# Delta net: learning rate and chunk decay spread over the heads by one float32r pass over stacked high and low rows

## The chip, the core and the metric

The kernel runs on one core of a Trainium2 chip. Its engines work side by side, each through its own list of instructions in order, and wait for each other by semaphores: PE (matrix products; its weight loads are shown as PEld), DVE (vector), ACT (scalar functions), POOL (GpSimd, a slower vector engine), and SP, which here only issues DMAs. The metric is the device time of one execution in microseconds, as the median of several. A lower number is better.

## The reference

The model has two blocks of two layers. The change is in the gated delta net ("GDN"), one of three mixers in each of the two layers of the second block, so it runs twice. There are 256 tokens, 8 heads of 64 channels and chunks of 64 tokens. What matters of it:

```python
def chunk_gated_delta_rule(q, k, v, g, beta):
    ...
    gc = jnp.cumsum(g, axis=-1)
    gamma = jnp.exp(jnp.where(causal, gc[..., :, None] - gc[..., None, :], -jnp.inf))
    kb = k * beta[..., None]
    m = jnp.where(strict, jnp.einsum('bnhid,bnhjd->bnhij', kb, k) * gamma, 0.0) + jnp.eye(c, dtype=jnp.float32)
    rhs = jnp.concatenate([v * beta[..., None], kb * jnp.exp(gc)[..., None]], axis=-1)
    sol = lax.linalg.triangular_solve(m, rhs, left_side=True, lower=True, unit_diagonal=True)
    ...
    q_dec = q * jnp.exp(gc)[..., None]
    k_dec = k * jnp.exp(gc[..., -1:] - gc)[..., None]
    chunk_dec = jnp.exp(gc[..., -1])
```

Per head and token there is one learning rate `beta` and one decay `exp(gc)`. Both multiply all 64 channels of their head. That is the "spreading" that the change is about.

## The kernel before

**Stages.** One program computes everything: the first block (to about 1120 us), then two delta-net layers. A layer (`layer`, L1846) runs the RWKV mixer and behind it the GDN mixer. The projections that other mixers need are cut into small pieces, and `fill()` puts such a piece between the steps of a mixer, so that PE has work while a mixer's chain goes through other engines. The order of each engine's list comes from a scheduler that estimates durations; it is fixed when the program is built.

**Weights.** Weights arrive in f32 (tile `wv`, DMA at L347). ACT casts them to float32r (`wh`, L375), DVE computes what the cast lost (`wl`, L376, called the residual below), and PE multiplies three times (L390, L391, L392). In the rows PE's operands all read f32, whether the matmul is full f32 or float32r. A full f32 matmul shows two records per instruction, a float32r one has one.

**Spreading before.** In `gdn`, `rows[32:40]` holds beta, 8 heads by 256 tokens. L1575 copies it into `b0`, a tile with the tag `inv_xt`; L1573 writes `eg`, the decay, in 8 rows of `alog`. A tag is a place in SBUF: a new tile with the tag waits until the readers of the former tile there are done. `selp` (tag `rw_e`, DVE copy at L1599) is a selector of 8 rows with ones where an output channel belongs to a head. The matmuls at L1603 (for `b0`) and L1652 (for `eg`), four each, contract over the 8 rows and give each channel its head's number, in full f32. L1604 and L1653 then multiply keys and queries by that.

**Inverses.** Both mixers solve a triangular system by `inverse_blocks` (L1165). The blocks go out by DMA and come back in `inv_t`; POOL then works through a chain of 30 small steps (L1184 a product, L1186 a sum), turns the result round into `inv_xt` (L1187), and DMAs carry it out (L1189) and back into place (L1197, tiles `rw_k`, `rw_v` and others, from `blocks`).

**RWKV's columns.** `column_tile` (L1272) takes 14 pieces of projection. Each has a tile `z` with the tag `rw_z`, two buffers in turn: POOL clears its first column (L1277), ACT fills it (L1278), DVE reads it (L1279). After the last column tile nothing else used `rw_z`.

**Around the change.** GDN's projection `gdn_proj` runs as fill work within RWKV: POOL clears three columns of `proj` (L1527), ACT copies (L1528) and scales (L1531), DVE convolves (L1533). RWKV's masks (L1418, L1419, DVE) follow scores on PE (L1415), whose next ones wait for them. L1242 and L1243 (ACT) take a logarithm of head sums and an exponential.

Of the kernel before, what the change touches and what calls it, by code (L numbers as in the profile page):

```python
# [11 lines left out]
F32 = mybir.dt.float32  # L12
F32R = mybir.dt.float32r
# [248 lines left out]
class Core:  # L262
# [1280 lines left out]
    def gdn(self, pool, i, c, qkv, gz, rows, alog, out, fill):  # L1543
        nc = self.nc
# [24 lines left out]
        df = self.sb(pool, [8, 4, 64], F32, "rw_ta", 2)  # L1569
        nc.vector.tensor_tensor(df, gcc[:, :, 63:64].to_broadcast([8, 4, 64]), gcc, op=ALU.subtract)  # L1570
        nc.scalar.activation(rows[64:72], df.rearrange("p c t -> p (c t)"), AF.Exp)
        eg = alog[:8]
        nc.scalar.activation(eg, gc, AF.Exp)  # L1573
        b0 = self.sb(pool, [8, 256], F32, "inv_xt")
        nc.vector.tensor_copy(b0, rows[32:40])  # L1575
        col = self.sb(pool, [128, 2, 72], F32, "rw_wa")
        p = self.psum()[:, :144].rearrange("p (c n) -> p c n", c=2)
        for cc in range(2):
# [16 lines left out]
        unit(k, 1.0, ("rw_k", "rw_v"))  # L1595
        fill()
        kb = self.sb(pool, S4, F32, "rw_lora")
        selp = self.sb(pool, [8, 4, 128], F32, "rw_e")
        nc.vector.tensor_copy(selp.rearrange("p n (h d) -> p (n h) d", h=2), self.ident[:8, :8, None].to_broadcast([8, 8, 64]))  # L1599
        for j in range(2):  # L1600
            p = self.psum().rearrange("p (n t) -> p n t", n=2)
            for n in range(2):
# [4 lines left out]
        both = self.sb(pool, [128, 2, 16, 64], F32, "rw_bkt")  # L1607
        gam, gat = both[:, 0], both[:, 1]
        selh = self.ident[:8, :8, None].to_broadcast([8, 8, 64])
        for cc in range(2):  # L1610
            p = self.psum().rearrange("p (h t) -> p h t", h=8)
# [36 lines left out]
        for j in range(2):  # L1648
            s = slice(2 * j, 2 * j + 2)
            p = self.psum().rearrange("p (n t) -> p n t", n=2)  # L1650
# [12 lines left out]
        for cc in range(2):  # L1663
            for src, o, w in ((v, vb, bcol), (k, ke, ecol)):
                p = self.psum()
# [9 lines left out]
        for ck in range(4):  # L1675
# [5 lines left out]
            if ck:  # L1681
# [3 lines left out]
                for hh in range(2):  # L1685
                    s = slice(64 * hh, 64 * hh + 64)
                    p = self.psum("acc").rearrange("p (n d) -> p n d", n=8)[rw, :4]
# [6 lines left out]
            p = self.psum("acc").rearrange("p (h d) -> p h d", h=8)[rw]  # L1694
# [4 lines left out]
            p = self.psum("acc").rearrange("p (n t) -> p n t", n=8)[:, :4]  # L1699
            for n in range(4):  # L1700
                for hh in range(2):
                    h = 2 * n + hh
# [6 lines left out]
            if ck < 3:  # L1709
                p = self.psum("acc").rearrange("p (n t) -> p n t", n=8)[:, :4]  # L1710
                for n in range(4):
                    for hh in range(2):
                        h = 2 * n + hh
# [648 lines left out]
```

## Time and profile before

| | us |
|---|---|
| runs | 3164.83, 3170.68, 3172.57 |
| median | 3170.68 |
| profiled execution, its own time | 3173.02 |
| its span, first to last instruction | 3171.1 |
| PE busy, PEld busy | 3062.1 (97%), 2569.1 (81%) |
| DVE, ACT, POOL busy | 2395.3 (76%), 1873.1 (59%), 151.4 (5%) |
| mean granted TensorE clock | 0.985 |

The profile is of one execution. An engine's busy time says how long it was working, not whether anyone waited for it; the chain of work is read from the rows of the timeline. There, a bracket at a row's end names how long its engine had been idle before and which instruction let it go on. Matmuls overlap in the pipeline, so their distance is read from start to start. The granted clock is a share of full speed: 1.00 is 2.4 GHz, 0.50 is 1.2 GHz.

### The profile page before, as it was taken

The numbers are of one execution on the slowest core, as the hardware profiler recorded it, in microseconds if no ns is written. First come the engines' busy times: TensorE is split into PE (matmuls) and PEld (weight loads), VectorE is DVE, ScalarE is ACT, GpSimd is POOL, SyncE is SP. The second block draws the span as 40 slices with busy tenths as digits, with TensorE's granted clock in tenths as the row PEclk, the third lists the DMA queues.
The fourth block names the chain that finished last, engine by engine and source line by source line (L and its number), as shares of the span: only waits on it lengthen the run. The fifth ranks groups of instructions, "written<-read, shape, count | busy, mean of one in ns | idle before, by whom it ended". The sixth has DMA issues, their size and how long they took to land. (4 is left out here: it accounts for less than half of the span.)

```text
span 3171.1 us, 48734 instructions
## 1 busy us (share of the span) xinstructions
PE 3062.1 (97%) x18724; PEld 2569.1 (81%) x18724; DVE 2395.3 (76%) x3811; ACT 1873.1 (59%) x2801; POOL 151.4 (5%) x285
## 2 busy tenths in 40 slices
PE   8988999999999989999999999999999999999998
PEld 7877688888878878888887888977888888888886
DVE  7677776766776677666666777579888888888886
ACT  5546555555455555545555555456777777777774
POOL 0000000000000011100000201000000000000000
PEclk9999999999999989999999999999999999999999
DMA  8425284451356134346843433488999999999993
GB/s 314 173 62 154 93 299 166 182 194 52 121 189 246 68 106 133 92 127 198 305 160 103 128 113 98 130 314 344 352 371 367 360 381 369 363 377 370 363 385 132
DMA packets 161085, 701.63 MB, mean 221 GB/s; under 512 B 41344, under 2 KB 55488, under 8 KB 97872
## 3 DMA queue, kind: packets, MB, share of 16 engines
q1 hardware_dynamic: 153984, 673.25, 58.4%
q0 software_dynamic: 6576, 24.98, 2.6%
q8 instruction: 148, 2.42, 0.3%
q14 instruction: 89, 0.73, 0.1%
q10 hardware_dynamic: 288, 0.25, 0.0%
HBM read 678.48 MB, written 19.94 MB: 220 GB/s over the span
## 5 line engine op out<-in xcount | busy, mean ns | idle before, releaser
L376 DVE TENSOR_TENSOR wl<-wv,wh 128x1024 fp32r<-128x1024 f32 (+1 forms) x808 | 970.5, 1212 | 380.4 <-ACT wh L375 369.4
L375 ACT CAST wh<-wv 128x1024 fp32r<-128x1024 f32 (+1 forms) x808 | 836.6, 1039 | 683.1 <-issue 207.7
L415 PE MATMUL bank<-xx,wh 128*128 128x512 f32 x1760 | 627.5, 399 | 5.1 <-ACT wh L375 2.4
L376 DVE TENSOR_TENSOR wx<-wv,ww 128x2048 fp32r<-128x2048 f32 x224 | 505.9, 2288 | 20.0 <-ACT ww L375 16.4
L416 PE MATMUL bank<-xx,wl 128*128 128x256 f32 x1760 | 494.0, 281 | 0.1
L375 ACT CAST ww<-wv 128x2048 fp32r<-128x2048 f32 x224 | 418.2, 1905 | 6.8 <-PE bank L392 3.8
L415 PEld LDWEIGHTS bank<-xx,wh 128*128 128x128 f32 x1760 | 331.2, 188 | 85.9 <-ACT wh L375 3.3
L390 PE MATMUL bank<-xx,wh 128*128 128x256 f32 x1120 | 338.9, 303 | 18.7 <-DVE xx L386 8.1
L416 PEld LDWEIGHTS bank<-xx,wl 128*128 128x128 f32 x1760 | 333.3, 189 | 5.3 <-DVE wl L376 0.6
L392 PE MATMUL bank<-xx,wl 128*128 128x256 f32 x1120 | 329.9, 295 | 7.0 <-DVE wl L376 6.9
L391 PE MATMUL bank<-xx,wh 128*128 128x256 f32 x1120 | 329.1, 294 | 0.0
L390 PEld LDWEIGHTS bank<-xx,wh 128*128 128x128 f32 x1120 | 222.4, 199 | 31.3 <-issue 17.8
L392 PEld LDWEIGHTS bank<-xx,wl 128*128 128x128 f32 x1120 | 222.6, 199 | 12.2 <-DVE wl L376 8.5
L391 PEld LDWEIGHTS bank<-xx,wh 128*128 128x128 f32 x1120 | 222.5, 199 | 6.1 <-issue 4.2
L390 PE MATMUL bank<-ww,xx 128*128 128x512 f32 x448 | 185.3, 414 | 0.0
L391 PE MATMUL bank<-wx,xx 128*128 128x512 f32 x448 | 178.1, 397 | 0.0
L441 PE MATMUL bank<-wh,hh 128*128 128x512 f32 x440 | 173.3, 395 | 4.6 <-ACT hh L375 4.5
L392 PE MATMUL bank<-ww,xx 128*128 128x512 f32 x448 | 177.4, 396 | 0.0
L390 PE MATMUL bank<-wh,xx 128*128 128x512 f32 x448 | 176.2, 393 | 0.0
L391 PE MATMUL bank<-wl,xx 128*128 128x512 f32 x448 | 175.8, 392 | 0.0
L392 PE MATMUL bank<-wh,xx 128*128 128x512 f32 x448 | 175.1, 391 | 0.0
L442 PE MATMUL bank<-wl,hh 128*128 128x512 f32 x440 | 172.2, 392 | 0.2 <-DVE wl L376 0.2
(667 smaller groups left out, 5363.8 us busy)
## 6 DMA issues: line engine op xcount, KB each, us to landing
wv<-in_moe_dram SPq DMA_DIRECT2D x336, 1024.0 KB, 7.2
wv<-in_ffn_dram SPq DMA_DIRECT2D x120, 1024.0 KB, 5.1
wv<-in_ffn_d_dram SPq DMA_DIRECT2D x30, 1024.0 KB, 5.7
wv<-in_in_t_dram SPq DMA_DIRECT2D x48, 512.0 KB, 3.7
wv<-in_in_g_dram SPq DMA_DIRECT2D x34, 512.0 KB, 4.1
wv<-in_in_r_dram SPq DMA_DIRECT2D x28, 512.0 KB, 3.7
wv<-in_ffn_dram SPq DMA_DIRECT2D x24, 512.0 KB, 4.5
wv<-in_br_dram SPq DMA_DIRECT2D x24, 512.0 KB, 4.0
```

Source lines behind the costliest of these rows:

```text
L375: self.nc.scalar.copy(h, v)
L376: self.nc.vector.tensor_sub(l, v, h)
L390: mm(out, l[0], r[0], start=start, stop=False)
L391: mm(out, l[0], r[1], start=False, stop=False)
L392: return mm(out, l[1], r[0], start=False, stop=stop)
L415: mm(out, w[0][:, k], self.xx[:, k], start=n == 0, stop=False, skip_group_check=True)
L416: mm(out[:, :256], w[1][:, k], self.xh[:, k], start=False, stop=n == nk - 1, skip_group_check=True)
L441: mm(p, x[0][:, s], w[0][:, c:c + n], start=first and r == 0, stop=False)
L442: mm(p, x[0][:, s], w[1][:, c:c + n], start=False, stop=False)
```

## The change

Each of `eg` and `b0` gets a new tile `both` of 40 rows in float32r, with the tag `rw_z`. POOL clears it, ACT casts the 8 rows into rows 0 to 7, and DVE writes what the cast lost into rows 32 to 39. The selector has 40 rows too, the same 8 at 0 and at 32; POOL clears and writes it, and DVE's copy falls away. One float32r matmul over 40 rows adds up the high and low parts. The number of matmul instructions is the same, and so are the tiles behind them.

```diff
@@ -1569,10 +1569,19 @@
         df = self.sb(pool, [8, 4, 64], F32, "rw_ta", 2)
         nc.vector.tensor_tensor(df, gcc[:, :, 63:64].to_broadcast([8, 4, 64]), gcc, op=ALU.subtract)
         nc.scalar.activation(rows[64:72], df.rearrange("p c t -> p (c t)"), AF.Exp)
+
+        spread = []
         eg = alog[:8]
         nc.scalar.activation(eg, gc, AF.Exp)
         b0 = self.sb(pool, [8, 256], F32, "inv_xt")
         nc.vector.tensor_copy(b0, rows[32:40])
+        for t in (eg, b0):
+            both = self.sb(pool, [40, 256], F32R, "rw_z", 2)
+            nc.gpsimd.memset(both.bitcast(F32), 0.0)
+            nc.scalar.copy(both[:8], t)
+            nc.vector.tensor_sub(both[32:40], t, both[:8].bitcast(F32))
+            spread.append(both)
+        eg, b0 = spread
         col = self.sb(pool, [128, 2, 72], F32, "rw_wa")
         p = self.psum()[:, :144].rearrange("p (c n) -> p c n", c=2)
         for cc in range(2):
@@ -1595,8 +1604,11 @@
         unit(k, 1.0, ("rw_k", "rw_v"))
         fill()
         kb = self.sb(pool, S4, F32, "rw_lora")
-        selp = self.sb(pool, [8, 4, 128], F32, "rw_e")
-        nc.vector.tensor_copy(selp.rearrange("p n (h d) -> p (n h) d", h=2), self.ident[:8, :8, None].to_broadcast([8, 8, 64]))
+        selp = self.sb(pool, [40, 4, 128], F32R, "rw_e")
+        nc.gpsimd.memset(selp.bitcast(F32), 0.0)
+        for n in (0, 32):
+            nc.gpsimd.tensor_copy(selp[n:n + 8].rearrange("p n (h d) -> p (n h) d", h=2),
+                                  self.ident[n:n + 8, n:n + 8, None].to_broadcast([8, 8, 64]))
         for j in range(2):
             p = self.psum().rearrange("p (n t) -> p n t", n=2)
             for n in range(2):
```

Line numbers up to L1571 are the same in both kernels; in the changed one the clear is L1580, the cast L1581, the residual L1582, and the lines behind move by 2, then by 9, then by 12.

On POOL, during RWKV's inverse in the first layer. Before (`rw_z_11995` and `rw_z_12030` are the tiles of RWKV's last two column tiles):

```order
L1277 MEMSET rw_z_11995 128x1
L1277 MEMSET rw_z_12030 128x1
L1184 ISA
L1184 TENSOR_TENSOR inv_m_11659<-inv_t_11653,inv_x_11655 128x15
L1186 TENSOR_TENSOR inv_x_11655<-inv_x_11655,inv_m_11659 128x15
L1184 TENSOR_TENSOR inv_m_11659<-inv_t_11653,inv_x_11655 128x28
```

After (`rw_z_13241` is the new tile for the decay):

```order
L1277 MEMSET rw_z_11995 128x1
L1277 MEMSET rw_z_12030 128x1
L1184 ISA
L1184 TENSOR_TENSOR inv_m_11659<-inv_t_11653,inv_x_11655 128x15
L1580 MEMSET rw_z_13241 40x256
L1186 TENSOR_TENSOR inv_x_11655<-inv_x_11655,inv_m_11659 128x15
L1184 TENSOR_TENSOR inv_m_11659<-inv_t_11653,inv_x_11655 128x28
```

The clear of the new tile, which takes the buffer of `rw_z_11995`, stands in the midst of the inverse, between its first product and its first sum. The clear of the second tile stands further down in the same chain; in the second layer both stand behind it.

On ACT, in the first layer, where GDN's projection begins. Before (`wh` and `wv` are weights, `proj` is GDN's projection, `rw_d` is RWKV's gate):

```order
L375 CAST wh_12204<-wv_12202 128x1024
L1399 COPY rw_d_12051<-bank_12052 128x512
L1399 COPY rw_d_12051<-bank_12056 128x512
L375 CAST wh_12278<-wv_12276 128x1024
L1528 COPY proj_12129<-bank_12098 128x256
L1531 ACTIVATE t_11325<-proj_12129,gd_cw_12062 128x256
L375 CAST wh_12341<-wv_12339 128x1024
```

After (`rw_z_13245` is the new tile for the learning rate, `inv_xt_13239` the copy of it):

```order
L375 CAST wh_12204<-wv_12202 128x1024
L1399 COPY rw_d_12051<-bank_12052 128x512
L1399 COPY rw_d_12051<-bank_12056 128x512
L1581 CAST rw_z_13245<-inv_xt_13239 8x256
L1528 COPY proj_12129<-bank_12098 128x256
L375 CAST wh_12278<-wv_12276 128x1024
L1531 ACTIVATE t_11325<-proj_12129,gd_cw_12062 128x256
L375 CAST wh_12341<-wv_12339 128x1024
L1528 COPY proj_12169<-bank_12138 128x256
```

The cast of the copied learning rate stands ahead of L1528 and of a weight cast that before came first.

## Rows read from the trace of the kernel before

**Rows 1.** page, part 1: busy us, share of the span, x instructions
```profile
PE 3062.1 (97%) x18724; PEld 2569.1 (81%) x18724; DVE 2395.3 (76%) x3811; ACT 1873.1 (59%) x2801; POOL 151.4 (5%) x285
```

**Rows 2.** timeline, PE: start, length, engine, line, operation, tiles, shapes, [idle before <-releaser]
```profile
1211.81 0.46 PE L1415 MATMUL bank<-x,rw_bkt 64*128 64x128 f32 x2 [2.34 <-DVE at_e L1419]
...
1295.46 1.13 PE L1603 MATMUL bank<-inv_xt,rw_e 8*128 8x256 f32 x4
1296.51 1.99 PE L1234 MATMUL bank<-rw_a,t 128*128 128x256 f32 x8
...
1301.40 0.71 PE L441 MATMUL bank<-wh,xx 128*128 128x416 f32 x1 [1.84 <-ACT rw_a L1242]
...
1331.10 0.28 PE L392 MATMUL bank<-xx,wl 128*128 128x256 f32 x1
1331.22 0.28 PE L390 MATMUL bank<-xx,wh 128*128 128x256 f32 x1
...
1910.66 0.46 PE L441 MATMUL bank<-wh,xx 128*128 128x416 f32 x1 [1.77 <-ACT rw_a L1242]
```

**Rows 3.** windows: length, busy us of each engine (x instructions), granted clock, DMA
```profile
1212.50:1213.00 0.50, 0.00 (x0) 0.00 (x0) 0.49 (x3) 0.38 (x3) 0.00 (x0) 0.54 0.37 34
1219.00:1219.50 0.50, 0.50 (x8) 0.28 (x9) 0.00 (x0) 0.00 (x0) 0.00 (x0) 0.64 0.28 115
...
1298.00:1300.00 2.00, 1.56 (x7) 0.77 (x5) 0.62 (x1) 1.97 (x3) 0.00 (x0) 1.00 0.00 0
...
1910.50:1911.00 0.50, 0.34 (x2) 0.34 (x3) 0.50 (x2) 0.50 (x2) 0.37 (x1) 1.00 0.00 0
```

**Rows 4.** timeline, DVE, both layers
```profile
1187.47 3.63 DVE L376 TENSOR_TENSOR wl<-wv,wh 128x1024 fp32r<-128x1024 f32 x3
1192.32 0.48 DVE L1279 SCALAR_TENSOR_TENSOR rw_v<-bank,t,rw_z 128x256 f32<-128x256 f32 x1 [1.22 <-POOL inv_x L1186]
...
1205.39 0.28 DVE L1575 COPY inv_xt<-t 8x256 f32<-8x256 f32 x1 [4.91 <-DMA blocks<-inv_xt]
1205.70 1.23 DVE L376 TENSOR_TENSOR wl<-wv,wh 128x1024 fp32r<-128x1024 f32 x1
...
1330.01 0.69 DVE L1653 TENSOR_TENSOR rw_b<-bank,rw_lora 128x512 f32<-128x512 f32 x1 [1.23 <-PE bank L1652]
...
1818.01 0.28 DVE L1575 COPY inv_xt<-t 8x256 f32<-8x256 f32 x1
1819.14 1.23 DVE L376 TENSOR_TENSOR wl<-wv,wh 128x1024 fp32r<-128x1024 f32 x1 [0.84 <-ACT wh L375]
```

**Rows 5.** timeline, POOL, first layer
```profile
1187.44 0.23 POOL L1186 TENSOR_TENSOR inv_x<-inv_x,inv_m 128x15 f32<-128x15 f32 x1
1187.75 1.09 POOL L1184 TENSOR_TENSOR inv_m<-inv_t,inv_x 128x28 f32<-128x28 f32 x1
...
1202.92 0.63 POOL L1187 COPY inv_xt<-inv_x 128x256 f32<-128x256 f32 x1
1204.69 0.31 POOL L1178 MEMSET inv_x<- 128x256 f32 x1 [1.14 <-DMA blocks<-inv_x]
...
1261.40 0.10 POOL L1527 MEMSET proj<- 128x3 f32 x1 [4.54 <-DVE t L1540]
```

**Rows 6.** timeline, ACT, first layer
```profile
1197.78 0.37 ACT L1520 ACTIVATE t<-bank 8x256 f32<-8x256 f32 x1
...
1202.02 1.05 ACT L375 CAST wh<-wv 128x1024 fp32r<-128x1024 f32 x1 [0.17 <-PE bank L391]
...
1265.00 0.51 ACT L1531 ACTIVATE t<-proj,gd_cw 128x256 f32<-128x256 f32 x1
```

**Rows 7.** waits of PE, 1790 to 2060: us in total, times, longest
```profile
PE bank L1214 <- DMA rw_k<-blocks: 2.3, 1, 2.3
PE bank L392 <- DVE wl L376: 2.2, 1, 2.2
...
PE bank L1466 <- DVE rw_k L1224: 1.1, 1, 1.1
```

## The prediction

> **What bounds the kernel now.** I read the page first: PE is busy for 97% of the span [rows 1], so the tempting reading is that every microsecond of matmul removed is a microsecond won. The timeline around the changed matmuls says otherwise, and I go by that. Times of the rows are microseconds from the span's start; the mixers of the first delta-net layer lie at about 1130 to 1440, those of the second at about 1740 to 2060.
>
> At the first spread (L1603) the two f32 matmuls of a pair take from 1295.46 to 1296.51, and behind the second pair PE stands still for 1.84 until ACT has read the sums of `rw_a` [rows 2]. ACT is busy there for 1.97 of 2 us [rows 3]: it is switching tables between logarithm and exponential. So ACT sets the pace here, not PE. At the second spread (L1652) it is DVE that waits, 1.23 [rows 4].
>
> A hundred microseconds earlier stands the place that I think decides. While RWKV's inverse runs on POOL, DVE sits idle for 4.91 before L1575, since the copy of the learning rate goes into the tile `inv_xt`, whose former contents a DMA has yet to send out [rows 4]; that DMA is issued when POOL's inverse is done. Behind this stall the masks of L1419 come late, and PE waits 2.34 for them at 1211.81 [rows 2]. POOL, busy for 5% of the span [rows 1], is thus on the path that sets the end here.
>
> **The matmuls.** Two f32 matmuls take 1296.51 - 1295.46 = 1.05, so 0.52 each; a float32r matmul of the same 256 columns starts 0.12 after the one before it, 1331.10 and 1331.22 [rows 2]. The stacked form contracts over 40 rows instead of 8 in one pass, so I give it 0.12 too: 0.40 less each, 16 of them (four for each of two spreads in each of two layers), 6.4 in all on PE.
> L1603: nothing comes of it in either layer. ACT is full, and PE only waits longer: the 1.84, and the 1.77 in the second layer [rows 2], become up to 3.4.
> L1652, first layer: four matmuls, 1.6 on PE; DVE waited 1.23 for the first pair [rows 4] and is the busier engine behind, so I take 1.0 of it (bounds 0 and 1.6).
> L1652, second layer: PE later waits 2.3 for a DMA of this mixer's own inverse (`rw_k` from `blocks`) [rows 7], and that chain began ahead of L1652; time won in front of such a wait is given back. I take 0.3 (bounds 0 and 1.6).
>
> **The clears on POOL, first layer.** The new tiles take over the two buffers of `rw_z`. The first one's clear stands on POOL right behind the first product of the inverse (the POOL order in the section on the change), and its buffer is the one that DVE's L1279 reads at 1192.32 for 0.48 [rows 4], so it can't start before 1192.80. The step that is now behind it began at 1187.44 [rows 5]. With a clear of 0.31, the price of L1178's with as many columns [rows 5], that step begins at about 1193.2: the chain is held by 5.8. Some of it comes back. Three residuals ran on DVE from 1187.47 on [rows 4], and beside them POOL's steps took 1.09 where 0.23 was the step before [rows 5]; now they run while POOL only waits, which gives back 3 x 0.86 = 2.6. The second clear, further down the chain, finds its buffer free and costs 0.35. Net 5.8 - 2.6 + 0.35 = 3.5 later for all that waits for this inverse (bounds 0, if the buffer is free sooner, and 6.1, if nothing comes back). In the second layer both clears stand behind the whole inverse and cost nothing.
>
> **The cast and the residual of the learning rate, first layer.** L1575 moves from 1205.39 to 1208.9. Then comes a step that was not there: ACT must cast the copy, and this cast stands ahead of L1528 and of the next weight cast L375 (the ACT order in the section on the change). Before, ACT did that weight cast during DVE's stall, at 1202.02 [rows 6]. Now ACT stalls too and works off afterwards: the copy on DVE 0.28 [rows 4], the cast 0.37 (as L1520, also 8x256), L1528 about the same, L375 1.05 [rows 6]. DVE's next weight residual starts at 1208.9 + 0.28 + 0.37 + 0.37 + 1.05, about 1211.0, instead of 1205.70 [rows 4]: 5.3 later. From there to the masks DVE has little slack, so PE's wait of 2.34 becomes about 7.6. Queued behind the cast on ACT are weight casts; the weights that PE multiplies at that time were cast earlier, so nothing else is late. First layer: +5.3.
>
> **The same in the second layer.** L1575 isn't held up, it runs at 1818.01, and DVE then waits 0.84 for a weight cast [rows 4]. The new cast goes in front of that one: 0.28 + 0.37, +0.65. The residual of the decay (`eg`), a DVE step priced between 0.28 (L1575) and 0.48 (L1279) [rows 4], goes ahead of L1224, for which PE's L1466 waits 1.1 [rows 7]: +0.4. In the first layer the copy L1599, which DVE loses, makes up for it: 0.
>
> **The selector on POOL.** One clear and two casts go where POOL had 4.54 idle before its last L1527 at 1261.40 [rows 5]; the reader of that one on ACT comes at 1265.00 [rows 6], 3.6 later. No row shows such a cast. By L1187's copy of 256 columns, 0.63 [rows 5], two of 512 are 2.5, and the clear 0.6; I take 0 (if the cover of 4.54 + 3.6 failed, each microsecond more would hold one activation). By the Trainium skill (SBUF — State Buffer, Who interferes with whom) a DVE instruction with two SBUF inputs shuts out one of GpSimd that reads SBUF, but not one that only writes it. The trace shows the first half: 1.09 against 0.23 beside the residuals [rows 4, 5]. By that rule each of the two casts may lose a whole residual of 1.22, and the clears nothing; the sum would still not leave the cover.
>
> **Order.** The scheduler also swaps some neighbours on PE, DVE and SP during the mixer's own inverse. I book 0; PE's longest wait for a residual in such a stretch, 2.2 [rows 7], is my bound to either side.
>
> **Sum.** +5.3 - 1.0 for the first layer, +0.65 + 0.4 - 0.3 for the second: +5.0. The profiled execution took 3173.02, so it would read 3178.1; it stands 2.3 above the median of 3170.68, and against that the forecast is 3175.7. That is +0.16%: slower, but within the 0.3% (9.5 us) below which a measurement of this kernel can't be told from no change.
>
> **Rivals.**
> (a) PE is what counts, and the clears hold nothing: all 6.4 are saved, 3164.3. For it: 97% busy [rows 1]. Against it: the waits of 1.84 and 1.77 [rows 2] and of 2.3 [rows 7], each behind a place where PE would be quicker, and the order on POOL. By the 0.3% it is no change either. 0.15.
> (b) Slower, by the clock. At the low level (granted clock 0.50, 1.2 GHz) PE's work takes twice as long. The clock fell between 1212.5 and 1213.0, after PE had waited for the masks, and was back between 1219.0 and 1219.5 [rows 3]: 6.5, of which half is lost where there is work. After the wait of 1.77 it was still 1.00 [rows 3]. With the waits at 1301 and 1910 grown towards 3.4 and that at 1211 to 7.6, low stretches may be longer or new: 3.3 lost at 1910 if it falls there as it did at 1212, and half as much, 1.65, at each of the other two, 6.6 together: 3182.3. It decides from the point where the wait at 1910 lets the clock fall. In my sum the clock is 0, because in the long wait of the first layer part of the low stretch passes while PE has nothing to do. 0.20. The Trainium skill (TensorE: Matmul & The Clock Gate, Why this matters for your kernels) warns of idle gaps between bursts of matmuls, because the array then drops to its cold clock; by that rule this rival would be the likeliest. The rows bear it out at 1212 and not at 1910.
> (c) The change doesn't do what it says: the stacked pass is no quicker than f32. Then the 1.3 gained at L1652 is missing, 3177.0. Nothing in the rows speaks for it, and 0.12 [rows 2] against it. 0.05.
>
> **Chances.** Forecast 0.60, (a) 0.15, (b) 0.20, (c) 0.05. The forecast's own ends: no hold (+1.8 in its place), both gains at L1652 whole and 2.2 from the order give 3168; a hold of 6.1, no gain and 2.2 against give 3182. The range 3165 to 3184 takes these in with (b), and leaves out (a) and little more. Faster than 3161.2 needs (a) and a lucky order: 0.04. Slower than 3180.2 is most of (b) and the upper end of the forecast: 0.20. Between them: 0.76.
>
> **What will show it.** Right: POOL's second step of the inverse in the first layer starts near 1193.2 and L1575 near 1208.9; PE's wait before L1415 is 7 to 8; PE's waits for `rw_a` grow to 2.5 or more in both layers, while the matmuls before them take a quarter of the time. Wrong: L1575 within a microsecond of 1205.4 (no hold); a wait for the masks that hasn't grown; or the gain at L1603 found again in an earlier L441. If the clock after the wait at 1910 is under 1.00, (b) has begun.

## The result and the profile after

The change made the kernel slower, by more than forecast: 3191.25 us against 3170.68, a ratio of 1.0062 (95% interval 1.0051 to 1.0074), 20.6 more. The forecast was 3175.7, with 3184 as the upper end. The profiled execution took 3189.01, its span is 3187.2, 16.1 more than before's 3171.1. The page, part 1 (busy us, share, instructions; beside [rows 1]):

```profile
PE 3054.2 (96%) x18708; PEld 2559.8 (80%) x18708; DVE 2396.9 (75%) x3813; ACT 1873.9 (59%) x2805; POOL 157.0 (5%) x295
```

PE does 7.9 less work than before, and the kernel is 16 longer: what was lost is mostly waits. To find them I took the start of every PE instruction that both kernels have, and looked at where the difference grows. It grows in few places: +5.4 between 1185 and 1290 (the front of the first layer), -2.3 up to 1330 (a little over half of it the quicker L1652, now L1664), +3.7 up to 1400 (the GDN mixer's inverse), +2.3 in the second layer's mixers, +5.2 behind the experts, and 1.8 in all the rest.

**The front went as forecast.** POOL's timeline of the kernel after (columns as in [rows 2]), beside [rows 5]:

```profile
1186.33 0.20 POOL L1184 TENSOR_TENSOR inv_m<-inv_t,inv_x 128x15 f32<-128x15 f32 x1
1191.97 0.30 POOL L1580 MEMSET rw_z<- 40x256 f32 x1 [5.43 <-DVE rw_v L1279]
1192.24 0.22 POOL L1186 TENSOR_TENSOR inv_x<-inv_x,inv_m 128x15 f32<-128x15 f32 x1
...
1263.86 0.53 POOL L1608 MEMSET rw_e<- 40x512 f32 x1 [1.83 <-DVE rw_k L1224]
1264.45 2.33 POOL L1610 CAST rw_e<-t 8x512 fp32r<-8x512 f32 x2
```

The clear waits 5.43 for DVE's L1279, and the inverse's second step stands behind it. DVE's timeline, beside [rows 4]:

```profile
1207.74 0.28 DVE L1577 COPY inv_xt<-t 8x256 f32<-8x256 f32 x1 [7.63 <-DMA blocks<-inv_xt]
1208.49 0.41 DVE L1582 TENSOR_TENSOR rw_z<-inv_xt,rw_z 8x256 fp32r<-8x256 f32 x1 [0.47 <-ACT rw_z L1581]
1209.70 1.22 DVE L376 TENSOR_TENSOR wl<-wv,wh 128x1024 fp32r<-128x1024 f32 x1 [0.80 <-ACT wh L375]
```

The stall grew from 4.91 to 7.63, and the weight residual behind it came at 1209.70 instead of 1205.70. PE's timeline, beside [rows 2]: the wait for the masks is 7.23 where it was 2.34, and the row of two stacked matmuls is 0.48 long where that of a pair in full f32 was 1.13.

```profile
1215.80 1.19 PE L1415 MATMUL bank<-x,rw_bkt 64*128 64x128 f32 x4 [7.23 <-DVE at_e L1419]
...
1300.14 0.48 PE L1615 MATMUL bank<-rw_z,rw_e 40*128 40x256 f32 x2
```

PE's waits around the first spread, 1294 to 1312: the time saved on the matmuls went into longer waits for ACT (1.84 before; the second layer's wait grew in the same way, from 1.77 to 2.5):

```profile
PE bank L441 <- ACT rw_a L1242: 2.5, 1, 2.5
PE bank L1234 <- ACT rw_a L1498: 0.5, 1, 0.5
```

Windows around the wait of 7.23 (length, busy time of PE, PEld, DVE, ACT, POOL, granted clock, DMA), beside [rows 3]: the clock fell to 0.50 in the wait, at 1211.1, and was back at about 1224.7. Before it was low for 6.8 (the prediction read 6.5), now for 13.6, of which PE stood still for the first 4.7.

```profile
1211.00:1211.50 0.50, 0.00 (x0) 0.00 (x0) 0.47 (x2) 0.28 (x2) 0.00 (x0) 0.55 0.34 32
...
1224.00:1224.50 0.50, 0.50 (x16) 0.50 (x13) 0.00 (x0) 0.00 (x0) 0.00 (x0) 0.50 0.00 0
1224.50:1225.00 0.50, 0.50 (x9) 0.43 (x6) 0.04 (x1) 0.00 (x0) 0.00 (x0) 0.79 0.00 0
```

**The clock also fell behind the longer wait in the second layer.** That wait of 2.5, which corresponds to the one at 1910 before, ends near 1919.6 in this execution. Windows around it: the clock was low from 1921.0 to 1924.4, with PE busy all the time, and the difference to before grew by 1.6 there. In the kernel before it was 1.00 behind this wait [rows 3], and stayed so up to 1917.

```profile
1919.00:1919.50 0.50, 0.00 (x0) 0.00 (x0) 0.50 (x2) 0.50 (x2) 0.50 (x1) 1.00 0.00 0
1920.50:1921.00 0.50, 0.50 (x4) 0.49 (x3) 0.00 (x0) 0.50 (x1) 0.00 (x0) 1.00 0.00 0
1921.00:1921.50 0.50, 0.50 (x3) 0.48 (x3) 0.00 (x0) 0.49 (x2) 0.00 (x0) 0.53 0.12 33
1924.00:1924.50 0.50, 0.50 (x3) 0.47 (x3) 0.50 (x3) 0.00 (x0) 0.00 (x0) 0.56 0.00 0
```

The kernel before was low a little later, from 1925.9 to 1929.3, where the one after was not, and 1.5 came back. From 1900 to 1990 both were low for 10.2 in all, at different places.

**Of the -2.3, the quicker matmuls are 1.2.** PE's timeline at the second spread, before:

```profile
1328.84 1.99 PE L1652 MATMUL bank<-t,rw_e 8*128 8x256 f32 x8
1330.76 0.39 PE L390 MATMUL bank<-xx,wh 128*128 128x256 f32 x1
```

and after:

```profile
1332.45 0.73 PE L1664 MATMUL bank<-rw_z,rw_e 40*128 40x256 f32 x4
1333.11 0.39 PE L390 MATMUL bank<-xx,wh 128*128 128x256 f32 x1
```

From the spread's start to the next matmul it is 1.92 before and 0.66 after. The other 1.1 lies ahead of it: before, the clock was low from 1318.4 to 1321.8 (windows of before), and in the execution after it was not.

```profile
1318.00:1318.50 0.50, 0.50 (x6) 0.50 (x5) 0.50 (x2) 0.00 (x0) 0.00 (x0) 0.85 0.82 332
1321.50:1322.00 0.50, 0.50 (x28) 0.50 (x32) 0.23 (x2) 0.47 (x2) 0.00 (x0) 0.74 0.03 8
```

The table of runs below agrees: e1 and e12, which have the quicker L1664 and also a low stretch here, gain 1.3 and 1.2 between 1290 and 1330, and e5 and e11, in full f32 without that stretch, gain 1.3 and 0.9.

**The GDN mixer's inverse did not.** SP's timeline of the kernel before (SP's rows are issues, and the length of a group reaches to its last one):

```profile
1325.06 4.92 SPq L1173 DMA_DIRECT2D blocks<-rw_bkt  x8
1330.56 0.34 SPq L1896 DMA_DIRECT2D gates<-gt  x1
1331.33 0.34 SPq L1175 DMA_DIRECT2D inv_t<-blocks  x1
```

and after:

```profile
1328.64 4.89 SPq L1173 DMA_DIRECT2D blocks<-rw_bkt  x8
1334.27 2.75 SPq L1908 DMA_DIRECT2D gates<-gt  x2
1337.23 0.32 SPq L1175 DMA_DIRECT2D inv_t<-blocks  x1
```

Two stores of gate tiles, not one, now stand between the blocks' way out and the load that starts POOL's chain, and the second waits for ACT. From the blocks' last issue to the load it was 1331.33 - 1329.98 = 1.35, now 1337.23 - 1333.53 = 3.70. PE feels it at the end of the chain. Its waits after, 1329 to 1398:

```profile
PE bank L1214 <- DMA rw_k<-blocks: 4.5, 1, 4.5
PE bank L392 <- DVE wl L376: 2.4, 1, 2.4
```

Before (1326 to 1392) it was

```profile
PE bank L1214 <- DMA rw_k<-blocks: 0.3, 1, 0.3
```

So the wait grew by 4.2. Of that 2.4 is the later load (3.70 against 1.35); the other 1.8 is time that PE had gained and now only waited: the 2.3 of above, less 0.5 that it lost again around 1335.

**The end was not in my sum at all.** PE's timeline before, at the first transposes behind the experts, and the transfers from 3134 to 3139.5 by queue (packets, MB, share):

```profile
3139.50 0.90 PE L555 MATMUL bank<-t,x 128*128 128x128 f32 x3 [5.37 <-issue]
```

```profile
q8 instruction: 1, 0.02, 1.1%
```

After, the same place, and the transfers from 3145 to 3156:

```profile
3156.10 1.12 PE L555 MATMUL bank<-t,x 128*128 128x128 f32 x4 [11.01 <-DMA wv<-in_ple_gate_dram]
```

```profile
q8 instruction: 2, 0.03, 1.3%
```

The wait is twice as long, and two pieces of instructions come in it instead of one. What lies between is a jump over a loop (`For_i(0, n)`, experts that overflow) that here runs zero times. The releaser that the trace names, the transfer of the gate weights, is doubtful: before, SP issued that transfer at 3140.74, when these transposes, which read `x`, had already begun (3139.50).

### The profile page after: what moved, and what is told of

Read it like the earlier page. It is cut to its first block, busy times and chain, and to the rows that moved or that the text cites. A ratio compares the mean times of both kernels' runs of the same rounds, so it can differ in the third digit from the quotient of the medians.

```text
span 3187.2 us, 48728 instructions
## 1 busy us (share of the span) xinstructions
PE 3054.2 (96%) x18708; PEld 2559.8 (80%) x18708; DVE 2396.9 (75%) x3813; ACT 1873.9 (59%) x2805; POOL 157.0 (5%) x295
## 5 line engine op out<-in xcount | busy, mean ns | idle before, releaser
L390 PE MATMUL bank<-xx,wh 128*128 128x256 f32 x1120 | 335.2, 299 | 19.4 <-DVE xx L386 7.8
L391 PE MATMUL bank<-xx,wh 128*128 128x256 f32 x1120 | 325.6, 291 | 0.0
L392 PEld LDWEIGHTS bank<-xx,wl 128*128 128x128 f32 x1120 | 218.8, 196 | 10.9 <-DVE wl L376 6.9
```

The costliest lines, as they stand in the source:

```text
L390: mm(out, l[0], r[0], start=start, stop=False)
L391: mm(out, l[0], r[1], start=False, stop=False)
L392: return mm(out, l[1], r[0], start=False, stop=stop)
```

## The experiments

e1 to e12 were timed in five rounds each beside the kernel before, whose median was 3171.1 to 3172.4 there. "Changed" is the changed kernel, "before" the one before.

| run | edit | us | ratio to before, 95% |
|---|---|---|---|
| after | the change | 3191.25 | 1.0062 (1.0051 to 1.0074) |
| e1 | changed, 16 tiny matmuls in the router | 3187.43 | 1.0055 (1.0038 to 1.0072) |
| e2 | changed, clears on DVE | 3185.39 | 1.0048 (1.0032 to 1.0064) |
| e3 | e2 without the copy | 3178.15 | 1.0022 (1.0010 to 1.0033) |
| e4 | changed, SP's order | 3183.22 | 1.0038 (1.0026 to 1.0050) |
| e5 | before, copy into `rw_z` | 3162.68 | 0.9972 (0.9960 to 0.9984) |
| e6 | e3 + e4 + e1 | 3176.88 | 1.0011 (1.0002 to 1.0020) |
| e7 | e3 + e4 | 3173.51 | 1.0001 (0.9988 to 1.0013) |
| e8 | changed, decay in f32 | 3180.24 | 1.0020 (1.0011 to 1.0029) |
| e9 | changed, tiny matmuls at the end | 3186.40 | 1.0041 (1.0028 to 1.0055) |
| e10 | e7 + tiny matmuls at the end | 3169.21 | 0.9991 (0.9981 to 1.0001) |
| e11 | before without the copy | 3166.23 | 0.9975 (0.9963 to 0.9986) |
| e12 | changed, learning rate in f32 | 3180.77 | 1.0029 (1.0016 to 1.0041) |

Where PE's instructions lie against before, by stretch of before's time (growth of the difference in us, one profile each; "rest" is everything else, where no edit acts directly; before 1000, in the first block, the runs alone differ by -5.1 to +2.1, and that is chance):

| run | front 1185-1290 | 1290-1330 | inverse 1330-1400 | 2nd layer 1800-2050 | experts 2150-3130 | end | rest |
|---|---|---|---|---|---|---|---|
| after | +5.4 | -2.3 | +3.7 | +2.3 | -0.1 | +5.2 | +1.9 |
| e1 | +6.6 | -1.3 | +2.7 | +3.2 | +4.0 | +0.2 | -0.9 |
| e2 | +2.5 | -2.3 | +3.6 | +3.0 | 0.0 | +6.0 | -3.2 |
| e3 | -4.7 | -2.2 | +3.9 | +1.0 | 0.0 | +5.0 | 0.0 |
| e4 | +5.4 | -2.3 | +0.4 | +2.0 | 0.0 | +5.1 | +0.6 |
| e5 | -1.6 | -1.3 | -2.7 | -0.5 | 0.0 | +0.5 | -4.8 |
| e6 | -4.9 | -2.2 | +1.2 | +2.3 | +3.7 | -0.1 | -2.1 |
| e7 | -4.6 | -2.2 | -0.9 | +1.9 | 0.0 | +6.2 | -2.9 |
| e8 | +6.6 | +0.1 | -2.6 | +2.1 | -0.1 | +0.2 | -1.6 |
| e9 | +6.8 | -1.1 | +3.9 | +3.5 | -0.1 | +0.5 | 0.0 |
| e10 | -4.9 | -2.2 | +0.5 | +1.7 | 0.0 | +0.1 | +2.9 |
| e11 | -4.9 | -0.9 | -2.8 | +0.6 | -0.1 | -0.1 | +3.3 |
| e12 | +3.1 | -1.2 | +3.5 | +1.4 | -0.1 | -0.1 | -4.1 |

The columns hold the clock as well, and a low stretch can differ between executions. e1 and e9 leave the front as the change has it, and lost 6.6 and 6.8 there, not 5.4, with the clock low for 17.1 instead of 13.6.

**e2, the hold.**
```
-            nc.gpsimd.memset(both.bitcast(F32), 0.0)
+            nc.vector.memset(both.bitcast(F32), 0.0)
```


> The changed kernel with the clears of the two stacked tiles on DVE instead of POOL; nothing else is changed. Theory H (hold): POOL's clear of the first stacked tile, which waits for the former reader of its buffer, holds RWKV's inverse in the first layer. Without it POOL's second step starts near 1187 instead of near 1192.7, the copy L1577 runs near 1204.5 instead of 1207.74, and of the 5.0 that the front of the first layer lost about 3.5 come back: offset to before +1.5 at 1223, time about 3187.5. Rival: the copy waits for the transfer that sends out inv_xt, and that is late for the queue it stands in, not for POOL; then L1577 stays near 1207.7 and the time at 3191.

POOL's and DVE's rows of e2 (this execution lies 2.4 earlier than the one after):

```profile
1183.90 0.20 POOL L1184 TENSOR_TENSOR inv_m<-inv_t,inv_x 128x15 f32<-128x15 f32 x1
1184.18 0.23 POOL L1186 TENSOR_TENSOR inv_x<-inv_x,inv_m 128x15 f32<-128x15 f32 x1
```

```profile
1202.27 0.28 DVE L1577 COPY inv_xt<-t 8x256 f32<-8x256 f32 x1 [4.55 <-DMA blocks<-inv_xt]
```

The second step follows the first at once, not 5.9 later, and DVE's stall is 4.55, near the 4.91 of before. The front loses 2.5 instead of 5.4, so the hold is worth 2.9 (3.5 forecast). The rival, a copy that stays late, falls.

**e12, the other part of the front.** `b0` is used as before (a copy in f32, `selp[:8]` read as f32); `both`, its clear, cast and residual are made for `eg` alone:
```
-        for t in (eg, b0):
+        for t in (eg,):
```


> The changed kernel with the other part undone: the learning rate's spread (L1615) in full f32 as before, without stacked tile, cast and residual; the decay's spread stays float32r, with its clear on POOL. Theory H: POOL's hold is still there (the decay's clear is the first in line) and the copy L1577 runs at about 1208, but no cast stands ahead of the next weight cast: the front loses about 3 instead of 5.4. SP's order is the changed kernel's (two gate stores ahead of the load), so PE's wait for rw_k stays near 4.5. Time 3186. Rival: the cast and the residual cost nothing of their own, the front still loses 5; or the hold does not cost, and it loses under 1.

POOL waits 5.44 for its clear again, the copy has 7.92 of idle time before it, and the front loses 3.1. So of 5.4 some 3 are the hold. The other 2.3 is the cast with its residual (1.7, read where PE's wait for the masks ends: the difference has grown by 4.9 there in the changed kernel, by 3.2 here) and a low clock that lasted longer (0.6). PE's wait for `rw_k` is 3.0 and not the 4.5 that I expected: in this execution the clock was low before L1664, as in the kernel before, and PE came later. The end has one fetch, and the time 3180.8 is lower than expected for that reason: this kernel's list of PE instructions isn't as short.

**e3, the stall itself.**
```
-        b0 = self.sb(pool, [8, 256], F32, "inv_xt")
-        nc.vector.tensor_copy(b0, rows[32:40])
-        for t in (eg, b0):
+        for t, hi, lo in ((eg, 0, 32), (rows[32:40], 32, 0)):
...
-            nc.scalar.copy(both[:8], t)
-            nc.vector.tensor_sub(both[32:40], t, both[:8].bitcast(F32))
+            nc.scalar.copy(both[hi:hi + 8], t)
+            nc.vector.tensor_sub(both[lo:lo + 8], t, both[hi:hi + 8].bitcast(F32))
```


> As the run with the clears on DVE, and the copy of the learning rate into a tile with the tag inv_xt is left out: the cast reads its 8 rows where they are, and its residual goes to the other 8 rows of the stacked tile. Theory H with the stall: without that copy nothing on DVE waits for the inverse's transfer, the 4.9 of idle time there disappear, RWKV's masks come in time, PE's wait of 2.3 before L1415 goes and with it the stretch at the low clock that followed it (6.5 long, half of it lost). Offset to before at 1223 between -3 and -6, time 3191 - 9 = 3182. Rival: the next thing in DVE's order needs the same inverse anyway, so the wait only moves; offset at 1223 about +0.5, time 3187.

DVE's timeline of e3, and two windows of it:

```profile
1199.66 0.41 DVE L1580 TENSOR_TENSOR rw_z<-t,rw_z 8x256 fp32r<-8x256 f32 x1
1202.07 1.23 DVE L376 TENSOR_TENSOR wl<-wv,wh 128x1024 fp32r<-128x1024 f32 x1 [2.00 <-ACT wh L375]
```

```profile
1200.00:1210.00 10.00, 9.11 (x81) 8.50 (x81) 7.79 (x15) 6.87 (x13) 3.78 (x11) 1.00 0.23 41
1210.00:1220.00 10.00, 10.00 (x112) 9.15 (x112) 7.03 (x16) 3.48 (x7) 0.20 (x2) 1.00 0.60 172
```

No stall for the transfer, no long wait for the masks, no low clock: the front is 4.7 shorter than before's, 10.1 shorter than the changed kernel's. DVE's stall was a price that the kernel before paid too.

**e5 and e11, that price alone.** e5 is before with one tag changed (the first cut below). e11 is before without the copy; its selector has the same ones in rows 0 to 7 and 32 to 39 (the second cut):
```
-        b0 = self.sb(pool, [8, 256], F32, "inv_xt")
+        b0 = self.sb(pool, [8, 256], F32, "rw_z", 2)
```


> The kernel before with one word changed: the copy of the learning rate goes into a buffer with the tag rw_z instead of inv_xt; both spreads stay in full f32. Theory H with the stall: DVE's 4.9 of idle time before that copy were a wait for a transfer that has nothing to do with it; without them PE's wait for RWKV's masks (2.3) and the low clock behind it go, as they did in the run with the cast read directly (4.9 there between 1185 and 1223). Time about 5 less than before: 3167, that is faster than the kernel before without any float32r. Rival: before's own GDN inverse and the order behind it give the time back further down (its wait for rw_k of 0.3 grows): 3171.

```
-        b0 = self.sb(pool, [8, 256], F32, "inv_xt")
-        nc.vector.tensor_copy(b0, rows[32:40])
+        b0 = rows[32:40]
...
+        selp = self.sb(pool, [40, 4, 128], F32, "rw_e")
...
+                mm(p[:, n], selp[32:, 2 * j + n], b0, start=True, stop=True)
```


> The kernel before without the copy of the learning rate, all in full f32: the selector gets a second set of 8 rows beside the learning rate's own rows, and its matmuls read both where they lie. Nothing on DVE or ACT is added but one copy of the selector. Theory: the stall that the copy caused (4.9 on DVE) is the price, whoever removes it gains; front of the first layer -2 to -5 to before (-1.7 in the run with the copy in another buffer, where the low clock stayed, -4.9 in the run with the direct cast, where it did not come), time 3162 to 3168. Rival: the gain of the other run came from chance in the first block (3 of its 10 us lay before 1000), and this one shows 3170.

Both beat both kernels in full f32, before by 0.28% and 0.25%: little, but beyond their intervals. e11 has the whole front (-4.9), e5 only 1.6 of it, because its clock was still low from 1209.4 to 1219.7, though PE waited for nothing longer than 0.9 there. Of e5's 10.2 in the profile 4.8 is in the rest, so chance helped it. Neither has the low stretch that before shows from 1352.5 to 1362.7 (-2.7 and -2.8 in the inverse's column); one profile of each can't tell whether that belongs to the edit. PE's wait for `rw_k` grew from 0.3 to 1.7 and 1.6, as the rival had it, and swallowed what PE had gained between 1290 and 1330. This is e5:

```profile
1340.00:1350.00 10.00, 5.99 (x43) 5.12 (x41) 9.39 (x33) 5.35 (x9) 1.38 (x5) 1.00 0.30 48
1350.00:1360.00 10.00, 9.80 (x165) 9.08 (x166) 8.18 (x29) 6.24 (x10) 0.00 (x0) 1.00 0.69 205
```

PE stood idle for 4 of 10 us there and kept the clock. Why it falls in one run's wait and not in another's stays open.

**e4, SP's order.**
```
-        nc.sync.dma_start(t16, dt)
+        self.loaded = nc.sync.dma_start(t16, dt)
...
-                    nc.sync.dma_start(gates[j], t)
+                    with self.tc.issue_after(self.loaded.ins):
+                        nc.sync.dma_start(gates[j], t)
```


> The changed kernel with every store of a gate tile made to stand behind the latest load of an inverse's blocks (inv_t) in SP's order. In the changed kernel two such stores stand between the blocks' way out and this load in the first layer, and the second of them waits for its tile. Theory S: that order is what delays the inverse in the first GDN mixer. Then the load is issued about 0.7 after the blocks are out (near 1334.3 instead of 1337.23), PE's wait for rw_k falls from 4.5 to about 1.6, and the offset to before at 1400 is about +4 instead of +6.3; time about 3189. Rival: the load would have waited for the blocks' transfer nearly as long, or another piece takes over (POOL beside DVE's residuals): offset at 1400 stays over +5.5, time 3191.

SP's timeline and PE's wait in e4:

```profile
1330.54 5.21 SPq L1173 DMA_DIRECT2D blocks<-rw_bkt  x8
1337.11 0.34 SPq L1175 DMA_DIRECT2D inv_t<-blocks  x1
1337.50 1.42 SPq L1909 DMA_DIRECT2D gates<-gt  x2
```

```profile
PE bank L1214 <- DMA rw_k<-blocks: 2.1, 1, 2.1
```

The load follows the blocks by 1.36 again, PE's wait falls by 2.4, and the inverse's stretch loses 0.4 instead of 3.7. Of these 3.3 the wait is 2.4; the rest goes with the clock, which was low for 3.4 here and for 6.8 in the changed kernel (1361.2 to 1368.1). So the order of two stores in SP's list was worth 2.4, and up to 3.3 with what the clock did. The medians differ by 8.0, the profiles by 4.9; these rows explain the profiles alone.

**e8, the decay's part undone.** The decay is used as before (`selp[:8]` read as f32); `both` is made for `b0` alone.
```
-        for t in (eg, b0):
+        for t in (b0,):
```


> The changed kernel with one part undone: the spread of the decay (L1664) in full f32 as before, its stacked tile, clear, cast and residual left out; the learning rate's spread stays float32r. In SP's order one gate store, not two, stands before the load of the inverse's blocks again. Theory S: PE's wait for rw_k in the first GDN mixer is back near 0.3 and what L1664 had saved (2.3) is missing, so from 1290 to 1400 the offset to before stays within 1 of what it was. Theory H: the learning rate's clear now is the first that asks for the buffer, so the hold stays and the front loses 5 as in the changed kernel. PE's list is 13 or so instructions shorter than before's, so whether the end needs the second fetch says on which side the piece's end lies; either may be. Time 3186 to 3191. Rival: the float32r spread of the decay is itself what costs, and the time falls to 3180 or less.

With L1664 slow, the scheduler puts one gate store, not two, ahead of the load, and PE's wait for `rw_k` is 0.7. The stretch from 1290 to 1400 reads -2.5, more than the "within 1" that I expected, since this run's clock stayed high from 1355 to 1365. The front loses 6.6: the hold is there whichever tile comes first. The time is under what theory H gave, 3180 against 3186 to 3191, and where the rival put it. The rows say why: against the changed kernel 5.0 came off at the end, which has one fetch, and 6.3 in the inverse's stretch, by the shorter wait and the higher clock. The front and the stretch up to 1330 are no quicker, so it isn't the stacked matmuls themselves that cost.

**e1 and e9, the end.** e1 adds to the twelve matmuls that keep PE warm in the router (`n == 12`), e9 to the eight behind the last expert (`n == 8`):
```
+            for _ in range(16 if n == 12 else 0):
+                self.nc.tensor.matmul(p[:, 0, :2], self.identb, self.identb[:, :2], start=True, stop=True)
```


> The changed kernel with 16 tiny matmuls (two columns each, results not used) added among those that keep PE warm in the router before the experts, where PE stands idle for 2.7 us. They bring PE's list of instructions back to about the length it had (the change took out 16 matmuls and 16 weight loads and added 3 semaphore waits). Theory F (instruction fetch): at the end PE jumps over code that is not run; the code behind the jump has to be fetched in pieces of 16 KB, and with a list that is 29 instructions shorter the first transposes (L555) fall on the far side of a piece's end, so PE waits for two pieces instead of one. Then the wait before the last L555 falls from 11.0 to about 5.4, the second fetch no longer stands before it, and the time is about 5.4 less than the changed kernel's 3191: about 3186. Rival D: PE waits there for the transfer of the gate weights, as the row of the trace names it, or the 5 us are chance of one run: the wait stays at 11 and the time at 3191, or the wait is short without a difference in the fetches.

> The changed kernel with the 16 tiny matmuls at another place: among the matmuls that keep PE warm behind the last expert, where the order of no other engine changes. (In the router they also moved ACT's casts in the experts, and a wait of 2.3 with a low clock behind it, 3.9 in all, appeared there.) Theory F: the experts stay as in the changed kernel (offset to before the same at 2150 and 3130), PE's wait before the last L555 is 5.2 to 5.6 with one fetch in front of it, and the time is 5 less than the changed kernel's: about 3186. Rival: a new wait takes the place of the second fetch, time 3191.

PE's timeline in e9, and the transfers of instructions from 3147 to 3153:

```profile
3152.76 3.67 PE L557 MATMUL bank<-t,x 128*128 128x128 f32 x16 [5.55 <-issue]
```

```profile
q8 instruction: 1, 0.02, 1.4%
```

Adding work took 5 us away: the wait is 5.55, one piece comes in it, and the median is 4.9 under the changed kernel's. All fourteen profiles agree. Counted in the traces (matmuls, weight loads, semaphore waits), PE has 37464 instructions ahead of this wait in the five kernels with two pieces (after, e2, e3, e4, e7; 10.9 to 11.3), and 37479 to 37496 in the nine with one (5.1 to 5.6). In e1 the end is cured as well (5.3), but its 16 matmuls also moved ACT's casts in the experts: PE waits 2.3 there for a residual at 2285, the clock falls, and 4.0 are lost. e6 has the same 2.3 and 3.7 at the same place.

**e6, e7 and e10, all together.** e7 is e3 with e4's edit, e6 adds e1's matmuls and e10 e9's.

> The changed kernel with all the repairs at once: clears on DVE, no copy of the learning rate, the gate stores behind the load of the inverse's blocks, and the 16 tiny matmuls in the router. If the four causes (POOL's hold, DVE's stall, SP's order, the fetch at the end) are separate, their prices add up: front -4.9 to before, PE's wait for rw_k in the first GDN mixer under 2, no second fetch before the last L555; about 6 less than before in the profile, 3166. If they hide one another, or the run with the tiny matmuls lost in the experts what it won at the end, then 3171 to 3175.

> The same without the 16 tiny matmuls. Theory F: it differs from its pair by the second fetch at the end alone, PE's wait there is 11 again and the time 5 more, 3171. Rival: the padding makes no difference in untraced runs, both the same within 2.

> All repairs of the changed kernel (clears on DVE, no copy of the learning rate, gate stores behind the load of the inverse's blocks), with the tiny matmuls behind the last expert. It differs from the run without padding only at the end, which had 3173.5, and whose end lost 5.9: theory F gives 3168, below the kernel before (3172). If the padding is worth nothing outside the profile, 3173.

e10 is 4.3 under e7, the fetch again; its profile has a wait of 5.1 where e7's has 11.3. e6 missed its forecast of 3166, and e7, which should have been 5 above it, is 3.4 below: e6 won 6.3 at the end, lost 3.7 in the experts and had the longer inverse. So padding is worth nothing where it moves other work. With everything repaired the float32r spread stands at 3169.21, level with before (0.9981 to 1.0001) and above the f32 versions e5 and e11: the idea itself gains nothing that these runs can tell.

## Why the prediction was wrong

By its own steps, profile against profile: forecast +5.0, measured +16.1. The miss of 11.1 is 5.2 at the end, 2.4 between 1290 and 1400 (forecast -1.0, measured +1.4), 1.6 in the second layer, and 1.8 in the rest, no more than the rest of other runs shows (2.0 of after's lies between 1400 and 1800, and no run takes it apart). The steps that failed are two: the order of the lists, put at 0 with a bound that looked at PE and DVE alone, and the code behind the mixers, which has no term at all.

- **L1603 saves nothing: right.** The difference is 4.61 on both sides of it, and the wait for ACT is 2.5.
- **Clears and cast, first layer, +5.3: right,** 5.4 measured. The mechanism is the one forecast: hold 3.5 forecast, 2.9 by e2; the masks' wait 7.6 forecast, 7.23 measured. That the sums agree to 0.1 is luck: the waits for the masks gave 4.9, and the longer low stretch, booked at 0, 0.6 here and more in e1 and e9.
- **Selector, 0: right.** POOL took 2.86 for it; the last L1527 came 5.45 later than before, of which 4.6 were lost earlier, and nobody waited.
- **L1652, first layer, gains 1.0: right in size, 1.2, but it was not kept.** It went into the wait for `rw_k`. I argued just this for the second layer, where the wait was 2.3, and not for the first, where the same wait was only 0.3. A wait of 0.3 means that PE and the chain are level, and what only PE gains is lost there: with SP's order put right, e4 still waits 2.1, and e5 and e11, where only the clock helped PE, wait 1.7 and 1.6.
- **"Order. I book 0": the first step that failed.** I bounded it by PE's longest wait for a residual, 2.2. It was SP's list that mattered, where a store that waits for its data now stood ahead of the load that starts a chain of 14 us: 2.4 of PE's wait by e4.
- **The end, +5.2, has no term: the second step that failed.** This is nearly half of the miss. I took it that code far behind the change can't change its time. The program has as many matmuls as before, but in PE's timeline a full f32 matmul is two (x8 for the four at L1652), each with its weight load, so by these PE's list is 29 instructions shorter (16 matmuls and 16 weight loads fewer, 3 semaphore waits more). As I read it, the code behind the jump now starts near the end of a fetched piece; where the pieces end isn't in the trace. A piece holds some 250 of PE's instructions (an estimate: 148 came on that queue before, for 2 x 18724 and 272 waits). e8 and e12, about half as much shorter, have one fetch: the edge lies between. The Trainium skill (Runtime: NRT & Kernel Launch, Instruction fetch mechanics) says that instructions are refilled in blocks of 16 KB and that a taken branch whose target isn't at hand stalls until its block has come. The trace agrees: 5.4 for one block, and 11.0 where a second one had to come.
- **Second layer, +0.75 forecast, +2.3 measured.** The cast's 0.65 is there (the difference goes from 8.12 to 8.75 between 1819 and 1821). The rest is a wait for `rw_k` of 5.0 where it was 2.3: POOL's chain took 14.9 instead of 13.4, beside DVE's residuals, and L1664 had gained 1.2 that was given back, as forecast for most of it. Every run with a float32r spread loses 1.0 to 3.5 in this stretch, the two without -0.5 and +0.6. This division is read from the rows and not tested by a run.
- **Rival (a)** is out: nothing of the 6.4 arrived. **Rival (b)** did begin, by its own sign: the clock after the wait that was at 1910 is 0.50 from 1921.0 to 1924.4. It cost 1.6 there, not 3.3, and made nothing of the sum, since the kernel before had as long a low stretch just behind; at 1301 the clock was low for 3.4 in both. All ten kernels with a stacked learning rate have this stretch, of the other four only e5. The longer low stretch at 1211 fell into the wait for a third, not for half. **Rival (c)** is out: 0.48 for two.
- The medians differ by 20.6, the profiles by 16.1. Some 2 are before's profile, which stands above its median, and as much after's, which stands below it.

## What to carry to other kernels

An edit changes the length of an engine's list, and so where the fetched pieces end: look at the first instructions behind every jump, even 1000 us behind the edit, and count the fetches there. Look for a moved instruction in the queue that starts a long chain, not only on the engine that you speed up, and treat a wait near zero as the end of what that engine can gain. And ask of the longest stall beside an edit what it is for: here the buffer of one copy cost the kernel before 4.9 at the front (e11), while the float32r spread brought nothing that these runs can tell.

## What had not been expected of the hardware

- 16 more matmuls made a kernel 4.9 faster (e9 against the changed kernel): behind a jump one piece of instructions came instead of two.
- The releaser of a wait can be wrong where an engine has no instructions: for the 11.01 before L555 the trace named a transfer that was issued only after L555 had begun in the kernel before.
- In e5 the granted clock fell at 1209.4 where PE had waited for at most 0.9, and stayed at 1.00 in e5 from 1340 to 1350 with PE idle for 4 of 10 us.
